# The first tile pair of a matrix product: A's rows by halves on both hardware queues, B's two tiles in column pieces by the software queue with a cast

## Chip, core and metric

The kernel runs on one core of a Trainium2 chip. The metric is the device time of one execution in microseconds (us); of the kernel before, eight runs are shown and their median is taken.

## What is computed

```python
def reference(a, b, gamma, eps):          # a, b: 2048 x 2048 fp32, gamma: 2048 fp32
    x = np.matmul(a, b)
    rms = np.sqrt(np.mean(x ** 2, axis=-1, keepdims=True) + eps)
    return (gamma * x / rms).astype(np.float32)
```

## The kernel before

**Tiles.** The 2048 rows of A make 16 row blocks of 128. The contraction of 2048 is cut into 16 tiles of 128 (`kt`), taken in 8 pairs (`kp`), so one pair covers 256 columns of A and 256 rows of B. The 2048 columns of B are two halves (`j`) of 1024. `raw[j][kp]` holds one pair of B for one half: 128 partitions, 2 tiles, 1024 columns, in bf16. A matmul takes a transposed 128x128 tile of A and 512 columns of B.

**The order of work is written out by hand** (`manual_schedule`): every engine runs its instructions in program order. There are three stages.

1. *The head.* Row blocks 0 to 3 times the left half of B, streamed by `kp`: 8 groups of (row block, 512 columns), of which seven keep a PSUM bank and the eighth is summed in parts (`stream_in_parts`, L415). For each `kp`, `stream` issues 14 matmuls (L384), and `transpose_head(kp + 1)` puts the next pair's 8 transposes (L172) in the middle of them; DVE copies the transposed tiles into `head_at` (L177).
2. *The right half of B* for the same four row blocks, again by `kp`.
3. *Row blocks 4 to 15* in pairs, with seven products in the place of eight (Strassen's scheme, L289), while ACT and DVE square, normalise and store earlier blocks.

**Who loads what.** `load_head(kp)` issues, on GpSimd's software queue, the pair of A for four row blocks (`early<-in_a_dram`, L105, 512 KB of fp32 read, cast to bf16) and the pair of B (`b<-in_b_dram`, L99, 1 MB of fp32 read, cast to bf16). The software queue has eight completion semaphores in turn, so the ninth load waits until the first has landed, the tenth until the second, and so on. Below, A1, B1, A2, ... are these loads for `kp` = 1, 2, ...

**The first pair (`kp` = 0) is loaded in another way.** A0 is one fp32 load on SP's hardware queue (L91), and B0's left half is two fp32 loads, one for each tile, on ACT's hardware queue (L93). They land in `a0f` and `b0f`, two parts of the tile `early`. `transpose_first` transposes A0 in fp32 on PE (L155, against `identity_f`, which GpSimd builds after it has issued A1 and B1), moves the result to `head_at` on DVE (L161), and casts B0 into `raw[0][0]` with DVE and ACT, half the columns each (L158, L160). The other loads of the head are issued by GpSimd before, between and after these.

Eleven matmuls on a zero tile (L145) keep PE busy until the first data come.

Of the kernel before, what the change touches and what calls it, by code (L numbers as in the profile page):

```python
# [8 lines left out]
FP32 = mybir.dt.float32  # L9
# [8 lines left out]
def kernel(  # L18
# [13 lines left out]
    nc = tc.nc  # L32
    P = 128
# [4 lines left out]
    W2 = 2 * P  # L38
    MB = M // P
    CH = 512  # L40
    NCH = N // CH
    HALF = N // 2
    HB = 4
# [15 lines left out]
    early = consts.tile([P, 6 * 2048], BF16, name="early")  # L59
    head_at = consts.tile([P, KT, HB, P], BF16, name="head_at")  # L60
    raw = [[consts.tile([P, 2, HALF], BF16, name=f"b_{j}_{kp}") for kp in range(KP)]
           for j in range(2)]
# [2 lines left out]
    sums = [t_left, t_right]  # L65

    a0f = early[:, 0:2048].bitcast(FP32).rearrange("p (r k) -> p r k", r=HB)
    b0f = [early[:, 2048 + t * 2048:2048 + (t + 1) * 2048].bitcast(FP32) for t in range(2)]
    NAH = 6
    ah_slot = [early[:, 6144 + s * 1024:6144 + (s + 1) * 1024].rearrange("p (r k) -> p r k", r=HB)  # L70
               for s in range(NAH)]
# [16 lines left out]
        return (at_even, at_odd)[(mb // 2) % 2][:, mb % 2]  # L88


    nc.sync.dma_start(out=a0f, in_=a[0:HB * P, 0:W2].rearrange("(r p) k -> p r k", p=P))  # L91
    for t in range(2):
        nc.scalar.dma_start(out=b0f[t], in_=b[t * P:(t + 1) * P, 0:HALF])  # L93

    def ah(kp):
        return ah_slot[(kp - 1) % NAH]

    def load_b(j, kp):
        nc.gpsimd.dma_start(  # L99
            out=raw[j][kp],  # L100
            in_=b[kp * W2:(kp + 1) * W2, j * HALF:(j + 1) * HALF].rearrange(
                "(t p) n -> p t n", p=P))

    def load_head(kp):
        nc.gpsimd.dma_start(  # L105
            out=ah(kp),
            in_=a[0:HB * P, kp * W2:(kp + 1) * W2].rearrange("(r p) k -> p r k", p=P))
        load_b(0, kp)
# [15 lines left out]
    def wait_for(src):  # L124

        nc.gpsimd.tensor_copy(out=pace, in_=src)

    load_head(1)
    identity_f = t_left[:, 2, KP - 1, 0:2 * P].bitcast(FP32)
    make_identity(nc, identity_f)  # L130
# [19 lines left out]
    def transpose_first():  # L150
        bank = [ps_t.tile([P, CH], FP32, name="tbank"), ps_a.tile([P, CH], FP32, name="acc")]
        view = [b.rearrange("p (r m) -> p r m", r=HB) for b in bank]
        for t in range(2):
            for r in range(HB):
                nc.tensor.matmul(view[t][:, r, :], a0f[:, r, t * P:(t + 1) * P], identity_f,  # L155
                                 is_transpose=True, start=(r == 0), stop=(r == HB - 1))
        for t in range(2):
            cast_first = [lambda: nc.vector.tensor_copy(out=raw[0][0][:, t, :CH],  # L158
                                                        in_=b0f[t][:, :CH]),
                          lambda: nc.scalar.copy(out=raw[0][0][:, t, CH:], in_=b0f[t][:, CH:])]  # L160
            move = [lambda h=h: nc.vector.tensor_copy(  # L161
                out=head_at[:, t, 2 * h:2 * h + 2, :], in_=view[t][:, 2 * h:2 * h + 2, :])
                for h in range(2)]
            for work in (cast_first + move if t == 0 else move + cast_first):
                work()

    def transpose_head(kp):
        bank = ps_t.tile([P, CH], FP32, name="tbank")
# [263 lines left out]
    for r in range(HB):  # L432
        x_tile(r, 0)
    early_sums = {4: ((2,), 0, 6), 5: ((5,), 0, 7), 6: ((1,), 0, KP)}
    transpose_first()
    for kp in range(KP):
        if kp + 4 < KP:
# [393 lines left out]
```

## Time and profile before

| | |
|---|---|
| median of 8 runs (lowest to highest) | 222.68 us (222.32 to 222.78) |
| the profiled execution: its time, its span | 222.68 us, 220.9 us |
| PE busy | 209.5 us, 95% of the span |
| DVE, ACT, POOL busy | 167.4, 128.0, 29.4 us |
| mean granted TensorE clock | 0.989 |
| software queue (q0): packets, MB | 9936, 23.33 |
| SP's hardware queue (q1), ACT's (q10): MB | 22.29, 1.31 |
| loads of B by POOL: count, KB written each, median issue to landing | 15, 512, 17.3 us |

The span is what the profile covers; about 1.8 us of the time lie around it. Start times in the profile count from the span's start. The DMA view counts bytes as written, so a load that casts fp32 to bf16 counts half of what it reads. A row of the timeline gives start, duration, engine, source line, operation, what is written and read, count, and in brackets the idle time just before it and what ended that. POOL is GpSimd, PEld is the weight load of a matmul; POOLq, SPq and ACTq are the issuing queues.

### The profile page before, as it was taken

How to read it: one execution, taken by the hardware profiler on the slowest of the kernel's cores; microseconds unless marked ns; L12 is line 12 of the kernel's file. 1: busy time of each engine (PE TensorE's matmuls, PEld its weight loads, DVE VectorE, ACT ScalarE, POOL GpSimd, SP SyncE). 2: the span in 40 equal slices, each digit the busy share in tenths (PEclk: the TensorE clock that was granted, in tenths of full speed). 3: DMA queues.
4: the chain of work that ended last, by engine and by line, in shares of the span. 5: the costliest groups of instructions: out<-in, count | busy, mean ns of one | idle time of the engine just before them, and what ended most of it. 6: DMA issues, size and time to landing. Idle time of an engine off the chain costs nothing.

```text
span 220.9 us, 3022 instructions
## 1 busy us (share of the span) xinstructions
PE 209.5 (95%) x1035; PEld 97.7 (44%) x1035; DVE 167.4 (76%) x330; ACT 128.0 (58%) x263; POOL 29.4 (13%) x59
## 2 busy tenths in 40 slices
PE   7899899999999999999999999999999999999950
PEld 2445444444455444444444444444444444444430
DVE  2428789999988898959697639855794759797691
ACT  3110002830698898479855997299738995334570
POOL 7634233220000002200010002000200000000040
PEclk9999999999999999999999999999999999999995
DMA  6999999999938595945799249955799349044045
GB/s 187 221 202 209 203 205 212 211 211 234 426 121 355 198 294 129 332 197 119 235 297 402 104 88 269 355 229 95 191 291 375 72 89 384 27 190 193 1 191 190
DMA packets 36321, 47.13 MB, mean 213 GB/s; under 512 B 21969, under 2 KB 26065, under 8 KB 34897
## 3 DMA queue, kind: packets, MB, share of 16 engines
q0 software_dynamic: 9936, 23.33, 41.6%
q1 hardware_dynamic: 25936, 22.29, 33.4%
q10 hardware_dynamic: 432, 1.31, 2.0%
q8 instruction: 8, 0.13, 0.2%
q14 instruction: 9, 0.07, 0.1%
HBM read 34.60 MB, written 16.78 MB: 233 GB/s over the span
## 4 chain that ended last, share of the span: by engine, by line
PE 83%; DMA 8%; POOL 3%; DVE 2%; issue 1%; ACT 1%; DVEq 0%; ACTq 0%; POOLq 0%
PE acc L289 69%; PE acc L384 12%; DMA b<-in_b_dram 8%; POOL early L105 1%; POOL b L99 1%; DVE x L709 1%; PE tbank L415 1%; PE tbank L172 1%; DVE x L712 1%; ACT sq L307 0%; PE tbank L189 0%; PE acc L189 0%; DVE a L709 0%; ACT sq L778 0%; DVE x L786 0%
## 5 line engine op out<-in xcount | busy, mean ns | idle before, releaser
L289 PE MATMUL acc<-b,s 128*128 128x512 bf16 x408 | 92.1, 379 | 0.0
L289 PEld LDWEIGHTS <-s 128*128 128x128 f16 (+1 forms) x512 | 49.9, 98 | 59.9 <-DVE s L264 0.4
L384 PE MATMUL acc<-b,head_at 128*128 128x512 bf16 x176 | 41.8, 379 | 0.8 <-DMA b<-in_b_dram 0.7
L307 ACT ACTIVATE sq<-x 128x512 bf16<-128x512 f32 x54 | 34.0, 630 | 6.9 <-DVE x L709 3.0
L366 DVE SCALAR_TENSOR_TENSOR x<-x,r,gamma_sb 128x1024 f32<-128x1024 f32 x28 | 34.8, 1281 | 0.7
L223 ACT ACTIVATE sq<-a 128x1024 bf16<-128x1024 f32 x24 | 25.3, 1054 | 3.2 <-DMA a<-in_a_dram 2.7
L384 PEld LDWEIGHTS <-head_at 128*128 128x128 bf16 x176 | 16.8, 98 | 20.3 <-issue 1.5
L246 ACT ACTIVATE head_at<-a,s 128x2048 f16<-128x2048 f32 x10 | 20.0, 1998 | 3.7 <-DVE s L233 3.7
L426 ACT COPY x<-acc 128x512 f32<-128x512 f32 x6 | 3.4, 588 | 25.4 <-PE acc L384 25.4
L289 PEld LDWEIGHTS <-head_at 128*128 128x128 f16 (+1 forms) x112 | 11.0, 98 | 13.2
L289 PE MATMUL acc<-early,head_at 128*128 128x512 bf16 x64 | 14.5, 379 | 0.0
L289 PEld LDWEIGHTS <-at_even 128*128 128x128 f16 x96 | 9.4, 98 | 11.3
L289 PE MATMUL acc<-early,s 128*128 128x512 bf16 x56 | 14.4, 379 | 0.0
L264 DVE TENSOR_TENSOR s<-head_at 128x1024 f16<-128x1024 f16 (+5 forms) x22 | 13.4, 637 | 0.1
L596 DVE TENSOR_TENSOR x<-x,x 128x512 f32<-128x512 f32 x9 | 6.2, 692 | 8.8 <-ACT x L594 8.3
L99 POOL DMA_DIRECT2D b<-in_b_dram x15 | 10.6, 706 | 15.9 <-DMA b<-in_b_dram 13.3
L578 ACT COPY x<-acc 128x512 f32<-128x512 f32 x9 | 5.2, 573 | 11.5 <-PE acc L289 7.6
L289 PE MATMUL acc<-t_left,s 128*128 128x512 bf16 x48 | 11.3, 379 | 0.0
L280 DVE TENSOR_TENSOR b<-b 128x1024 bf16<-128x1024 bf16 x16 | 10.9, 692 | 0.2
L289 PE MATMUL acc<-early,at_even 128*128 128x512 bf16 x48 | 10.8, 379 | 0.0
L289 PE MATMUL acc<-t_left,head_at 128*128 128x512 bf16 x48 | 10.8, 379 | 0.0
L289 PE MATMUL acc<-t_left,at_even 128*128 128x512 bf16 x48 | 10.8, 379 | 0.0
(111 smaller groups left out, 216.6 us busy)
## 6 DMA issues: line engine op xcount, KB each, us to landing
out_dram<-x SPq DMA_DIRECT2D x30, 512.0 KB, 3.8
a<-in_a_dram POOLq DMA_DIRECT2D x10, 1024.0 KB, 8.7
b<-in_b_dram POOLq DMA_DIRECT2D x15, 512.0 KB, 17.3
a<-in_a_dram POOLq DMA_DIRECT2D x4, 512.0 KB, 16.6
early<-in_a_dram POOLq DMA_DIRECT2D x7, 256.0 KB, 14.7
early<-in_b_dram ACTq DMA_DIRECT2D x2, 512.0 KB, 6.0
gamma_sb<-in_gamma_dram POOLq DMA_DIRECT2D x1, 1024.0 KB, 14.8
early<-in_a_dram SPq DMA_DIRECT2D x1, 512.0 KB, 5.6
```

Of the source, the lines that this page charges most:

```text
L99: nc.gpsimd.dma_start(out=raw[j][kp], in_=b[kp * W2:(kp + 1) * W2, j * HALF:(j + 1) * HALF].rearrange("(t p) n -> p t n", p=P))
L223: nc.scalar.activation(out=junk, in_=a32[mb][:, h * HALF:(h + 1) * HALF], func=ACTF.Square, scale=2.0 ** -8, accum_out=n2[:, h:h + 1])
L246: nc.scalar.activation(out=a16[mb], in_=a32.pop(mb), func=ACTF.Copy, scale=factor.pop(mb))
L264: nc.vector.tensor_tensor(out=sum_of(g, s)[:, lo:hi, :], in0=x[:, lo:hi, :], in1=y[:, lo:hi, :], op=op)
L280: nc.vector.tensor_tensor(out=flat[:, 1:3, :], in0=flat[:, 1:3, :], in1=flat[:, 0::3, :], op=ALU.add)
L289: nc.tensor.matmul(bank, lhsT[:, kp, :], rhs, start=(start and kp == 0), stop=(kp == KP - 1), skip_group_check=not start)
L307: nc.scalar.activation(out=sq[:, 0:CH], in_=src, func=ACTF.Square, scale=inv_sqrt_n, accum_out=msq[mb][:, c:c + 1])
L366: nc.vector.scalar_tensor_tensor(out=x, in0=x, scalar=inverse_of[mb], in1=gamma_sb[:, h * HALF:(h + 1) * HALF], op0=ALU.mult, op1=ALU.mult)
L384: nc.tensor.matmul(bank, head_at[:, kt, r, :], head_rhs(c, kt), start=(kt == 0), stop=(kt == KT - 1))
L426: copy(out=x_chunk(*g), in_=banks[g])
L578: nc.scalar.copy(out=c, in_=one[1])
L596: nc.vector.tensor_tensor(out=t, in0=t, in1=x12, op=ALU.add)
```

## The change

A0 becomes two loads of 256 KB, row blocks 0 and 1 on SP's queue and row blocks 2 and 3 on ACT's. B0 no longer passes through `b0f`: four loads on the software queue, ahead of `load_head(1)`, each 256 columns of both tiles, are cast to bf16 on the way into `raw[0][0]`. The casts by DVE and ACT go, and ACT takes the moves to `head_at` of the second tile, which DVE had.

```diff
-    b0f = [early[:, 2048 + t * 2048:2048 + (t + 1) * 2048].bitcast(FP32) for t in range(2)]
...
-    nc.sync.dma_start(out=a0f, in_=a[0:HB * P, 0:W2].rearrange("(r p) k -> p r k", p=P))
-    for t in range(2):
-        nc.scalar.dma_start(out=b0f[t], in_=b[t * P:(t + 1) * P, 0:HALF])
+    for h, queue in enumerate((nc.sync, nc.scalar)):
+        queue.dma_start(out=a0f[:, 2 * h:2 * h + 2, :],
+                        in_=a[2 * h * P:(2 * h + 2) * P, 0:W2].rearrange("(r p) k -> p r k", p=P))
...
+    for c in range(4):
+        col = slice(c * W2, (c + 1) * W2)
+        nc.gpsimd.dma_start(out=raw[0][0][:, :, col],
+                            in_=b[0:W2, col].rearrange("(t p) n -> p t n", p=P))
     load_head(1)
     identity_f = t_left[:, 2, KP - 1, 0:2 * P].bitcast(FP32)
     make_identity(nc, identity_f)
...
-        for t in range(2):
-            cast_first = [lambda: nc.vector.tensor_copy(out=raw[0][0][:, t, :CH],
-                                                        in_=b0f[t][:, :CH]),
-                          lambda: nc.scalar.copy(out=raw[0][0][:, t, CH:], in_=b0f[t][:, CH:])]
-            move = [lambda h=h: nc.vector.tensor_copy(
-                out=head_at[:, t, 2 * h:2 * h + 2, :], in_=view[t][:, 2 * h:2 * h + 2, :])
-                for h in range(2)]
-            for work in (cast_first + move if t == 0 else move + cast_first):
-                work()
+        for t, copy in enumerate((nc.vector.tensor_copy, nc.scalar.copy)):
+            for h in range(2):
+                copy(out=head_at[:, t, 2 * h:2 * h + 2, :], in_=view[t][:, 2 * h:2 * h + 2, :])
```

The matmuls and transposes on PE keep their number and order. After the change GpSimd issues four loads more before it builds `identity_f`, and the ninth load of the software queue is A3 in the place of A5.

## Prediction

> **What bounds the kernel now.** PE is busy for 95% of the span, so I first read the chain of waits: it should be PE work to the end, and the question is where it begins. By line, and in order of time:
>
> ```profile
> PE 83%; DMA 8%; POOL 3%; DVE 2%; issue 1%; ACT 1%; DVEq 0%; ACTq 0%; POOLq 0%
> ```
> ```profile
> 6.69 0.65 POOL early L105
> 7.35 17.46 DMA b<-in_b_dram
> 24.80 0.04 issue
> 24.84 1.67 PE acc L384 x7
> 26.52 0.45 PE tbank L172 x8
> ```
>
> From 24.84 us to about 208 us PE waits for nothing of length. Before that the end is not set by PE's start at 7.6 us, but by one load of B, landing at 24.80. The timeline shows the same from PE's side:
>
> ```profile
> 6.46 0.63 PE L155 MATMUL tbank<-t_left,early 128*128 128x128 f32 x4 [0.94 <-DMA early<-in_a_dram]
> 7.61 2.81 PE L384 MATMUL acc<-b,head_at 128*128 128x512 bf16 x12
> 11.65 0.59 PE L415 MATMUL tbank<-b,head_at 128*128 128x512 bf16 x2 [0.35 <-DVE head_at L177]
> 12.28 1.67 PE L384 MATMUL acc<-b,head_at 128*128 128x512 bf16 x7
> ...
> 24.84 1.67 PE L384 MATMUL acc<-b,head_at 128*128 128x512 bf16 x7 [0.71 <-DMA b<-in_b_dram]
> ```
>
> A `kp` takes PE 3.90 us (starts at 12.28, 16.18, 20.07). The next would be 23.97; it is 24.84, so 0.87 us are lost to B4. The trace's landing records give B1 12.24, B2 16.02, B3 19.96, B4 24.80, B5 28.62, B6 32.54, B7 36.37, against PE's starts 12.28, 16.18, 20.07, 24.84, 28.74, 32.64, 36.54: PE runs 0.04 to 0.17 us behind the software queue all through the head. On the right half of B the last landing, 56.25, is followed by its use at 56.40. So the head is paced by the **software queue**, and PE gains from an earlier start only what that queue gains.
>
> Third, the DMA view by stretches: 0 to 8 us, 2 to 6.3 us, then 8 to 12 us (columns: packets, MB written, share of 16 engines).
>
> ```profile
> q10 hardware_dynamic: 278, 1.04, 46.6%
> q1 hardware_dynamic: 528, 0.52, 19.8%
> q0 software_dynamic: 99, 0.05, 4.6%
> ```
> ```profile
> q10 hardware_dynamic: 181, 0.68, 55.8%
> q1 hardware_dynamic: 528, 0.52, 36.8%
> ```
> ```profile
> q0 software_dynamic: 849, 0.81, 122.8%
> q10 hardware_dynamic: 10, 0.01, 0.8%
> ```
>
> GpSimd issues A1 at 1.25 us, yet until 6.3 us q0 has moved nothing (first packet in the records at 6.53), and until 8 us only 0.05 MB. A0 and B0, as fp32 on the hardware queues, hold the engines until 8.0 us. After that q0 runs at 0.81 MB in 4 us, 0.203 MB/us.
>
> **What the Trainium skill says.** "DMA: Bandwidth & Descriptors", section Issuing engines are not separate DMA queues: loads from all queues run on the same 16 engines and interleave. The trace agrees on the sharing, but q0 gets no packet from 2 to 6.3 us, so here hardware queues go first; I use the measurement. Same page, SWDGE vs HWDGE vs iDMA: only the software queue casts. The trace agrees: B0 on ACT's queue is fp32 and needs L158 and L160. "SBUF — State Buffer", section SBUF: two separate sides: DVE's wide copies can block GpSimd from writing descriptors. I see none of it: the issue at 5.63, beside DVE's cast, took 0.73 us, others 0.70.
>
> **The change part by part.**
>
> *The software queue's stream (sets the end).* Before, its bulk begins at 8.0 us with 0.05 MB done, as if it had begun at 8.0 - 0.05/0.203 = 7.75. After, the hardware queues carry only A0, 0.52 MB. From 0 to 4.3 us they moved 0.6 MB before, ramp included (the packet records reach 0.52 MB at about 4.1), so I take 4.1 us as their end; 3.7 if 1 KB rows go at 0.3 MB/us, as from 4.3 to 6.3, from 2 us on, 4.6 if the ramp is longer. Then q0 carries B0: 0.524 MB at 0.203, 2.6 us, and A1 follows at 6.7. The stream is ahead by 7.75 - 6.7 = **1.05 us** (1.45 to 0.55). The source of the gain: B0 as fp32 on ACT's queue moved 0.33 MB from 6.3 to 8 us, about 0.2 MB/us as written, no faster than q0, which writes half the bytes for it.
>
> *Supply on q0.* Issues start at 1.25, 2.18, 2.88, 3.58 (pitch of L105 and L99 before: 0.93 for the first, then 0.70); A1 4.28, B1 5.04. On idle engines q0's first packet came 1.3 us after its issue (issue 64.04, packet 65.36), so each is ready before 6.4. A2 moves from 3.42 to 6.3, B2 to 7.1, A3 and B3 to about 8 to 9, A4 and B4 to about 10 and 11. A3 to B4 now wait for the four pieces, landed by 7.4; A5 waits for A1 as before. q0 needs A2 only at 6.7 + 3.9 = 10.6. Free.
>
> *`identity_f`.* GpSimd builds it after four more issues: 2.86 us later by the pitches, 3.47 + 2.86 = 6.33. A0 lands well before (6.33 in the landing records before, sharing with B0; now some 4.6). The first transposes start at 6.4 instead of 6.46. Cost nothing; what was covered by A0 is now the limit. PE is idle from 5.5 to 6.4 as it was.
>
> *Moves and casts.* DVE's two casts (0.71, 0.43 us) and ACT's two (0.62 each) go. The cast of B0's second tile ended at 9.3, and PE's matmuls show a 0.05 us gap there: gain 0.05. DVE's moves of the first tile (0.38 us each) follow the transposes as before; ACT's two, estimated at 0.4 us from L160's 0.62 for 512 columns, run at 7.2 to 8.0 and are wanted at 8.8, when the seventh group takes their bank, and 9.0. Free.
>
> *PE's start.* Transposes at 6.4 put the first matmul at 7.55 against 7.61. It needs pieces 0 and 1, the next also 2 and 3: last byte at 6.7, plus 0.7 (B1's last byte at 8.0 + (0.786 - 0.05)/0.203 = 11.6, landing 12.24) is 7.4. With the 0.05 gap and B1's wait (0.2) gone, PE could reach `kp` 4 at 24.84 - 0.87 - 0.2 - 0.05 - 0.06 = 23.66, 1.18 us sooner; B4's landing allows 24.80 - 1.05 = 23.75. The loads decide: 1.05 us, later slacks (0.10 to 0.17 us) add nothing. SP's queue has nothing else until the first store, and ACT's has one load less.
>
> *Sum.* Against the profiled execution, 222.68 us with a span of 220.9 and equal to the median: 222.68 - 1.05 = **221.6 us**. PE's own limit bounds the gain at about 1.25.
>
> **The rivals.** *A: the software queue starts late by itself* (slower). That q0 carries nothing before 6.53 us might not be the hardware queues' doing, but a first start that takes 5.3 us. B0 then has no other way in. q0's bulk begins at about 6.5, B0 is through at 9.1, the stream is 9.1 - 7.75 = 1.35 us late, the first matmul comes at 9.8: 224.0 us. It decides from the point where q0's bulk begins after 5.15 us (7.75 - 2.6). For it: no first start without hardware traffic is in the trace, and at 6.5 us q0 ran beside q10 while at 5 us it didn't beside q1. Against it: an issue at 88.96, beside stores on q1, got its first packet after 4.4 us, while quiet ones took 1.3. 16 in 100.
>
> *B: the stream gains little.* A0 by halves ramps more slowly and holds the engines until 4.7 to 5.15 us, or GpSimd's pieces take 0.93 us each like the first issue, so `identity_f` comes at 7.0 and PE's own start gives back half. Gain 0 to 0.45: 222.3 to 222.7. For it: 0.2 MB was all that moved before 3.3 us. Against it: that stretch was mostly 4 KB rows. 11 in 100.
>
> *C: the change as described does not happen*, as when the pieces were issued behind A1: the program shows them first on POOL. No share.
>
> **How the numbers follow.** A measurement of this kernel can tell about 0.2%, 0.45 us, from no change. Forecast, faster by 0.45 to 1.4 us: 73 in 100. B within 0.2%: 11. A slower by over 0.2%: 16. The forecast's own range is 221.3 to 222.2. The range reaches into A, whose mild cases (bulk at 5.6 to 5.7) give 223.2, and is cut below at 221.2, just past PE's limit: 221.2 to 223.2.
>
> **What would show it.** Right: q0's first packets at about 4 us and hardware traffic gone by then, B0's pieces landed by 7.4, A1 landed near 8.7 (before 9.71), PE's first matmul near 7.5, PE at `kp` 4 near 23.8 with a short wait or none, and the same 184 us from there to the end. Wrong: q0 silent until 6 us with idle engines; a matmul wait for a piece of B0 past 8.6 us; `identity_f` past 7 us; or a new wait behind `kp` 4, which would take the gain back later.

## The result, and the profile after

The changed kernel takes 223.88 us (median of 11 runs, 223.40 to 225.06) against 222.52 us (31 runs): ratio 1.007, 95% interval 1.0056 to 1.0084. It is slower by 1.4 us where 1.05 us less was forecast.

Its runs form two groups. The six at 223.4 to 223.9 us have a mean granted TensorE clock of 0.988 to 0.994; those at 224.7 to 225.1 have 0.980 or 0.981. One run lies outside this pairing, 224.57 us at 0.991, so a low clock is not all that can make a run long. The profiled execution is of the second group: 224.68 us, span 222.9 us. It took 2.00 us more than the profiled execution before.

The chain of waits by engine, of the changed kernel, and the same chain in order of time (start, duration):

```profile
PE 90%; DVE 3%; DMA 2%; POOL 1%; ACT 1%; issue 1%; DVEq 0%; ACTq 0%; POOLq 0%
```
```profile
1.24 2.21 POOL b L129 x3
3.45 0.12 issue
3.57 5.54 DMA b<-in_b_dram
9.11 0.05 issue
9.15 4.23 PE acc L381 x11
```

DMA's share fell from 8% to 2%, but the load that now sets PE's course is B0 itself. The fourth piece is issued at 3.57 us and lands at 9.11. After it the chain is nearly all PE to the end; the wait at `kp` 4 is gone.

The timeline of PE:

```profile
6.41 0.66 PE L158 MATMUL tbank<-t_left,early 128*128 128x128 f32 x4 [0.28 <-POOL t_left masks.py:199]
6.90 0.60 PE L158 MATMUL acc<-t_left,early 128*128 128x128 f32 x4
7.58 0.39 PE L381 MATMUL acc<-b,head_at 128*128 128x512 bf16 x1
9.15 4.23 PE L381 MATMUL acc<-b,head_at 128*128 128x512 bf16 x11 [1.19 <-DMA b<-in_b_dram]
...
15.05 1.67 PE L381 MATMUL acc<-b,head_at 128*128 128x512 bf16 x7
```

The transposes now wait for POOL's identity, and the first matmul runs at 7.58 as forecast. The second needs columns 512 to 1023 and waits for them until 9.15. Then eleven matmuls take 4.23 us, where twelve took 2.81 before. The windows view shows why (after the busy times: granted clock, DMA share, GB/s):

```profile
8.00:10.00 2.00, 0.84 (x3) 0.30 (x4) 0.00 (x0) 0.18 (x1) 2.00 (x11) 0.80 1.38 198
10.00:12.00 2.00, 2.00 (x6) 0.71 (x5) 0.00 (x0) 0.00 (x0) 1.74 (x3) 0.50 1.15 208
12.00:14.00 2.00, 2.00 (x15) 1.13 (x14) 0.13 (x1) 0.00 (x0) 0.70 (x1) 0.84 1.34 202
```

From 10 to 12 us PE runs at half clock. The same stretch before, at full clock:

```profile
10.00:12.00 2.00, 1.65 (x14) 0.93 (x13) 0.69 (x1) 0.00 (x0) 0.77 (x1) 1.00 1.16 203
```

Between the end of its warm-up at 6.13 us and the second matmul at 9.15 PE was busy for about half of the time, 1.48 of 3.02 us; its longest pause there was 1.19 us.

The DMA view of the changed kernel from 0 to 8 us, from 4 to 8, and from 8 to 12 us:

```profile
q0 software_dynamic: 970, 0.47, 59.4%
q1 hardware_dynamic: 272, 0.26, 10.0%
q10 hardware_dynamic: 272, 0.26, 9.3%
```
```profile
q0 software_dynamic: 853, 0.41, 105.8%
```
```profile
q0 software_dynamic: 918, 0.81, 126.2%
```

The hardware queues are through early: A0's two halves have landed at 3.90 and 4.17 us. The software queue has its first packet at 3.41. But from 4 to 8 us it moves 0.41 MB, 0.10 MB/us; only from 8 us on does it reach 0.203. In the first stretch the engines are busy all the time (105.8%), so they aren't short of work: each packet takes longer. In the packet records one of 512 B takes 77 ns on average from 4 to 6 us and 90 ns from 6 to 8, against 60 ns from 8 to 10, and fewer of them overlap.

### The profile page after: what moved, and what is told of

Its sections match the earlier page's. It is cut to its first block, busy times and chain, and to the rows that moved or that the text cites. A ratio compares the mean times of both kernels' runs of the same rounds, so it can differ in the third digit from the quotient of the medians.

```text
span 222.9 us, 3025 instructions
## 1 busy us (share of the span) xinstructions
PE 211.6 (95%) x1035; PEld 98.2 (44%) x1035; DVE 165.4 (74%) x326; ACT 127.4 (57%) x263; POOL 32.2 (14%) x63
## 4 chain that ended last, share of the span: by engine, by line
PE 90%; DVE 3%; DMA 2%; POOL 1%; ACT 1%; issue 1%; DVEq 0%; ACTq 0%; POOLq 0%
PE acc L286 68%; PE acc L381 18%; DMA b<-in_b_dram 2%; PE tbank L412 2%; PE tbank L169 1%; POOL b L129 1%; DVE x L706 1%; DVE x L709 1%; ACT sq L304 0%; PE tbank L186 0%; PE acc L186 0%; DVE head_at L174 0%; DVE a L706 0%; ACT sq L775 0%; DVE x L783 0%
## 5 line engine op out<-in xcount | busy, mean ns | idle before, releaser
L381 PE MATMUL acc<-b,head_at 128*128 128x512 bf16 x176 | 43.6, 391 | 1.3 <-DMA b<-in_b_dram 1.2
L98 POOL DMA_DIRECT2D b<-in_b_dram x15 | 10.6, 709 | 14.9 <-DMA b<-in_b_dram 11.9
L174 DVE COPY head_at<-tbank 128x1024 bf16<-128x1024 bf16 x7 | 4.8, 686 | 8.7 <-PE tbank L169 8.7
L125 POOL COPY pace<-x 128x1 f32<-128x1 f32 x4 | 1.6, 412 | 65.9 <-DVE x L602 64.7
```

Of the source, the lines that this page charges most:

```text
L98: nc.gpsimd.dma_start(out=raw[j][kp], in_=b[kp * W2:(kp + 1) * W2, j * HALF:(j + 1) * HALF].rearrange("(t p) n -> p t n", p=P))
L174: nc.vector.tensor_copy(out=head_at[:, 2 * kp:2 * kp + 2, :, :], in_=view)
L381: nc.tensor.matmul(bank, head_at[:, kt, r, :], head_rhs(c, kt), start=(kt == 0), stop=(kt == KT - 1))
```

## Experiments

Landing times below are the last of a load's sixteen completions in the trace. "Stream" is how much later than before the last load of B's right half lands (56.25 us before). Where one time stands alone, the kernel ran once, and the time is set beside 222.68 us of the profiled execution before. What is read from such a run is its trace.

### Which part costs

**x7: the pieces without A0's halves.**

```diff
-    for h, queue in enumerate((nc.sync, nc.scalar)):
-        queue.dma_start(out=a0f[:, 2 * h:2 * h + 2, :], in_=...)
+    nc.sync.dma_start(out=a0f, in_=a[0:HB * P, 0:W2].rearrange("(r p) k -> p r k", p=P))
```

> The changed kernel with the other part alone: A0 as one load on SP's queue, the pieces of B0 on the software queue. A0 on one queue needs until about 4 us in the place of 3.7, still well before GpSimd has built the identity at 6.3 us; the pieces land near 9.1 to 9.5 us and the time is that of the changed kernel, 223.4 to 225 us. The two halves of A0 are then worth nothing in the changed kernel.

Measured: 223.88 us, ratio 1.0059 (1.004 to 1.0077), A0 landed at 4.09 us, the last piece at 9.96. The same median as the changed kernel: the pieces cost, and the halves of A0 give nothing beside them.

**x6: A0's halves without the pieces.**

```diff
-    nc.sync.dma_start(out=a0f, in_=a[0:HB * P, 0:W2].rearrange("(r p) k -> p r k", p=P))
+    for h, queue in enumerate((nc.sync, nc.scalar)):
+        queue.dma_start(out=a0f[:, 2 * h:2 * h + 2, :], in_=...)
     for t in range(2):
         nc.scalar.dma_start(out=b0f[t], in_=b[t * P:(t + 1) * P, 0:HALF])
```

> The kernel before with one part of the change: A0 by halves on both hardware queues, and B0 as fp32 behind it on ACT's queue, cast by DVE and ACT as before. If reading B0 is what is slow, at 0.2 MB/us as read, A0 can no longer hide beside it: the hardware queues end near 3.7 + 1.05/0.2 = 9 us against 8.0, the stream of the software queue comes 0.9 us later, the time is about 223.4 us. If the slowness of the pieces belongs to the software queue, B0 goes at 0.3 MB/us or more, the hardware queues end near 7.2 us and the time is about 221.9 us.

Measured: 223.37 us, ratio 1.0045 (1.002 to 1.007); B0's second tile landed at 10.39 us against 8.68 before. The loss of the first guess, but not by its reason: before the software queue began, ACT's queue moved 0.33 MB of B0 from 3.5 to 4.5 us. q0 got its first packets at 4.8 us, with 0.62 MB still to come on ACT's queue; from 5.5 to 6.5 us both together moved 0.12 MB. So neither reading of the expectation holds as written. Two things follow: the slowness falls on both queues and not on the software queue alone, and the hardware queue did not go first here, though the prediction assumed that it does.

**x12: only B0's second tile on the software queue, in one load.**

```diff
-    for t in range(2):
-        nc.scalar.dma_start(out=b0f[t], in_=b[t * P:(t + 1) * P, 0:HALF])
+    nc.scalar.dma_start(out=b0f[0], in_=b[0:P, 0:HALF])
...
+    nc.gpsimd.dma_start(out=raw[0][0][:, 1, :], in_=b[P:W2, 0:HALF])
     load_head(1)
...
-            for work in (cast_first + move if t == 0 else move + cast_first):
+            for work in (cast_first + move if t == 0 else move):
```

> The kernel before with only B0's second tile moved: A0 whole on SP's queue and B0's first tile as fp32 on ACT's queue as before, the second tile by one software load with a cast, ahead of A1, and its two casts gone. The hardware queues end near 5.9 us in the place of 8.0; PE starts at 7.6 as before and wants the second tile at 9.1. At full rate the stream is ahead by 8.0 - (5.9 + 1.3) = 0.8 us: 221.9 us. If the software queue's first 0.26 MB go at 0.11 MB/us, they take 2.4 us, the stream is 0.3 us late: about 222.9 us, with PE not waiting for the tile (it lands near 8.9).

Measured: 222.78 us, ratio 1.0009 (1.0002 to 1.0017). The second reading: the tile landed at 8.74 us, PE didn't wait for it, B1 landed at 12.61 against 12.24. Half the bytes by the software queue cost a fifth of the loss. No version here beats the kernel before.

### Why the pieces are slow

**x1: the first two row pairs swapped; x5: the pieces read from A; x8: a small load that touches B's rows first; x2: one load in the place of four.**

```diff
 x1   in_=b[W2:2 * W2, col] for the pieces, b[0:W2, ...] for B1, A's columns likewise
 x5   in_=a[HB * P:HB * P + W2, col].rearrange("(t p) n -> p t n", p=P)
 x8 + nc.sync.dma_start(out=early[:, 2048:2112]..., in_=b[0:W2, 0:16]...)   ahead of A0
 x2 - for c in range(4): ...
 x2 + load_b(0, 0)
```

> The changed kernel with the first two row pairs of the contraction swapped: the first pair is columns 256 to 511 of A with rows 256 to 511 of B, the second is the old first. (Row blocks 4 to 15 keep A's natural order, so their products for these two pairs mix the wrong operands; no instruction or size differs.) Theory PLACE: the first 256 rows of B read slowly, about 0.11 MB/us as written, wherever they stand in the order. Then the four pieces land by about 7.4 us (the prediction's rate) and it is B1 that takes twice its 2.5 us. Theory FORM: the pieces themselves (1 KB rows, 512 B written, four loads in a row) are slow: unchanged, last piece near 9.1 us. Theory FIRST: the first loads of the software queue are slow whatever they are: also unchanged, 9.1 us.

> The changed kernel with the four pieces read from A (rows 512 to 767, columns 0 to 1023) in the place of B's first rows; A's other loads have touched that matrix by then, those rows not. (B0's left half is so wrong data; sizes, row pitch and order are the same.) Theory TOUCH-B: the first megabyte read from the matrix B is slow, whoever reads it. Then the pieces move at 0.2 MB/us and land near 7 us, and B1, now the first read of B, takes 4.5 us in the place of 2.5. Theory PATTERN: a first read of 256 rows of 4 KB at 8 KB pitch is slow from any matrix: unchanged, last piece near 9.1 us.

> The changed kernel with one small load more, first on SP's queue: 64 bytes of each of B's first 256 rows, into a place that is not used. Theory TOUCH-B in its form by rows or pages: the touch takes the first-read cost, the pieces then move at 0.2 MB/us from 3.6 us on and land near 7 us. If it is bytes that are slow and not the first touch, nothing changes but some 0.3 us for the load itself: last piece near 9.1 to 9.4 us.

> The changed kernel with B0 as one software load of 256 rows x 1024 columns (4 KB rows read, 2 KB written), the same form as B1 to B7, in the place of the four pieces. Theory FORM: B0 lands at about 3.6 + 2.6 + 0.7 = 7 us, the stream is 1.0 to 1.5 us ahead of before, the time is about 221.5 us. Theories FIRST and PLACE: B0's 0.52 MB still take some 4.5 us from 3.5 us on and land near 9 us, the time stays near 223.4 us or above.

Measured, last landing of B0: x1 9.49 us, x5 9.38, x8 9.57, x2 9.17 (the changed kernel: 9.11). x1, x5 and x8 ran once each: 224.14, 224.99, 224.99 us; x2 225.12 us, ratio 1.0127 (1.011 to 1.0144). From 4 to 8 us of x5, and from 4 to 7 of x2, the DMA view gives:

```profile
q0 software_dynamic: 873, 0.42, 100.8%
```
```profile
q0 software_dynamic: 185, 0.38, 101.6%
```

It is not these rows (x1), not the matrix (x5), not a first touch of the rows (x8, which touched 64 B of each), and not the 1 KB rows of the pieces (x2): a load of the form of B1 to B7 goes at 0.13 MB/us in this stretch. x2 is worse than the pieces in the median: four of its six runs had the clock near 0.98 (224.8 to 225.6 us), the other two took 223.3 and 223.6. PE's first matmul then waits for the whole of B0, from 6.4 to 9.21 us in its profile, which is of one of these two.

**x4: A1 ahead of the pieces; x9: A1 to A4 ahead of them; x10: GpSimd held back by six memsets, so that the software queue starts later.**

```diff
 x4 + nc.gpsimd.dma_start(out=ah(1), in_=a[0:HB * P, W2:2 * W2]...)     ahead of the pieces
 x9 + for kp in range(1, 5): load_a(kp)                                 ahead of the pieces
x10 + for n in range(6): nc.gpsimd.memset(x_slot[n], 0.0)               ahead of the pieces
```

> The changed kernel with A1's load (512 B written per row, as the pieces) issued on the software queue ahead of the four pieces of B0. Theory FIRST: A1 is now the slow one, 0.26 MB at about 0.11 MB/us, landing near 6.5 us, and the pieces speed up as time passes. Theory FORM or PLACE: A1 moves at 0.2 MB/us and lands near 5.6 us, and the four pieces still take 4.5 us, landing near 10.3 us. The time is in both cases longer than that of the changed kernel, by 1 us or more, since B0 comes later.

> The changed kernel with the loads A1, A2, A3 and A4 ahead of the four pieces of B0 on the software queue, so that the pieces move at about 9 us and later in the place of 3.6. Theory EARLY: what the software queue moves before 8 or 9 us is slow, whatever it is. Then the A loads are slow (0.11 to 0.16 MB/us) and the pieces, once the A loads are through, take 0.52/0.2 = 2.6 us. Theory FIRST-B: the first load of B's form is slow (0.11 MB/us, 4.5 us) whenever it comes. The whole is much longer than the changed kernel (by 5 us or more), since B0 comes last.

> The changed kernel with six memsets of 128x1024 fp32 on GpSimd ahead of the pieces, so that the software queue's very first load starts several us later, with nothing else in flight. If slow is a window in time from the kernel's start (to 8 or 9 us), the pieces now move at 0.2 MB/us. If slow is the first use of the queue (its first 4 to 5 us), they move at 0.11 MB/us as before. Longer than the changed kernel by the delay.

Measured: x4, 224.53 us: A1 landed at 6.77, the last piece 3.9 us later: first in line is slow, and the pieces behind it still are. x9, 230.62 us: A4 landed only at 11.90, 1.05 MB in over 8 us, and the four pieces 2.7 us after it, at full rate (first fence below, 11.9 to 14 us). x10, 229.36 us: first packets after 7.5 us, the pieces landed from 9.14 to 14.17. The second fence has 8 to 13 us of x10:

```profile
q0 software_dynamic: 628, 0.41, 134.3%
```
```profile
q0 software_dynamic: 1152, 0.56, 102.6%
```

0.11 MB/us, long after the time at which the changed kernel was at full rate. So no clock time ends the slowness, and the form of B0 is not its cause (x9). What these runs share is that the slow stretch follows the software queue's first packets: it lasts from them to about 8 us in the changed kernel (4.6 us) and to about 12 us in x9 (8.5 us, with one faster microsecond in between). x10 has a second one, from about 15 to 18 us, after a microsecond at full rate.

**x11, x13, x14: GpSimd quiet while B0 moves.** x11 keeps the four pieces; x13 has one load; x14 is x13 with memsets in the place of rest.

```diff
-    load_head(1)
     ...
     make_identity(nc, identity_f)
 x14 + for n in range(7): nc.gpsimd.memset(x_slot[n % 4], 0.0)
+    nc.gpsimd.tensor_copy(out=quiet, in_=raw[0][0][:, 1, HALF - 1:HALF])
+    load_head(1)
```

> The changed kernel with GpSimd building the identity right behind the pieces and then waiting until the last piece has landed, before it issues A1, B1 and the rest: while the pieces move, GpSimd writes no descriptors. Theory DESCRIPTORS: writing descriptors for the next loads slows the engines' work on the pieces; then they move at 0.2 MB/us from 4.5 us on and land by about 7 us. Otherwise they still land near 9 us. The time is longer than the changed kernel's, since A1 and B1 are issued late.

> The changed kernel with B0 as one software load (one issue of 0.9 us), then the identity, then GpSimd idle until B0 has landed; A1, B1 and the rest follow. While B0 moves, no descriptor at all is written. Theory DESCRIPTORS (the engines are slow while GpSimd writes descriptors): 0.52 MB at 0.2 MB/us from 3.6 us, landing near 7 us, against 9.17 us for the same load with GpSimd writing on. Theory START (the software queue's loads are slow for some us after it begins from rest): landing near 8.5 to 9 us all the same. The time is longer than the changed kernel's, since A1 is issued late.

> As the run before it (B0 as one software load, the rest of the loads held back until it has landed), with seven memsets of 128x1024 fp32 on GpSimd while B0 moves, in the place of rest. If any writing by GpSimd slows the engines, B0 lands as late as beside descriptor writing, near 9 us. If it is the descriptors, B0 lands as in the run before it.

Measured: last landing of B0 in x11 8.19 us, in x13 9.06, in x14 8.97; times 228.81, 231.25, 229.99 us, mostly because A1 and B1 come late (B1 lands at 17.48, 19.57 and 18.67 us). The row of GpSimd that waits for B0 in x13:

```profile
9.12 0.18 POOL L131 CAST quiet<-b 128x1 f32<-128x1 bf16 x1 [6.38 <-DMA b<-in_b_dram]
```

For 6.38 us GpSimd writes no descriptor, and the load is as slow as in x2 (9.17). That descriptor writing slows the engines falls as the whole cause. As a part of it, it doesn't fall: the first of the load's sixteen completions came at 6.46 us against 7.34 in x2, and x11 was 0.9 us quicker than the changed kernel. With one trace of each, how much of that is chance stays open. After the rest the queue starts again; A1 is then quick, and B1 is slow again: it lands 6.8 us after A1 in x13 and 5.8 in x14, against 2.5 before.

**x15: the kernel before, with the software queue at rest until the hardware queues are done.**

```diff
+    for n in range(7): nc.gpsimd.memset(x_slot[n % 4], 0.0)
     load_head(1)
```

> The kernel before with seven memsets of 128x1024 fp32 on GpSimd ahead of A1's load, so that the software queue is at rest until about 7.5 us, while A0 and B0 are on the hardware queues as before. If it is the start of the software queue that slows all 16 engines, the hardware queues, which ended at 8.0 us in the kernel before, now end near 6 to 6.5 us, and B0's second tile moves at 0.3 MB/us or more in the place of 0.2. If the two are independent, the hardware queues end at 8.0 us again. The time is longer by the delay of A1, some 5 us.

Measured: 225.81 us. The DMA view from 5.5 to 7 us, x15 first, then the kernel before:

```profile
q10 hardware_dynamic: 126, 0.46, 75.4%
q1 hardware_dynamic: 37, 0.03, 5.9%
```
```profile
q10 hardware_dynamic: 74, 0.30, 78.2%
q1 hardware_dynamic: 51, 0.04, 9.0%
```

With no software load issued, ACT's queue moves 0.46 MB where it moved 0.30, and B0's second tile lands at 7.48 us in the place of 8.68. The hardware queues end at about 7.1 us, between the two times of the expectation. So issuing loads on the software queue slows the hardware queues too, though q0 moves almost nothing in this stretch; whether it is the waiting loads or the writing of their descriptors, this run doesn't tell. When q0 then begins, for the first time in this kernel, A1 is quick (first packet 8.60, landed 10.79) and B1 lands 5.4 us later. A first start, then, does not make the very first load slow in every case.

### The clock

**x3: a longer warm-up.**

```diff
-    for _ in range(11):
+    for _ in range(16):
         nc.tensor.matmul(warm_bank, warm[:, 0:P], warm[:, 0:CH], start=True, stop=True)
```

> The changed kernel with 16 matmuls on the zero tile in the place of 11, so that PE stays busy until about 7 to 8.3 us. Theory GATE: the changed kernel's runs fall into two groups, near 223.4 and near 224.9 us, because in some executions PE's wait for B0 falls into a window in which its clock is cut to half. With the longer warm-up nearly all runs are in the lower group: median about 223.4 (223.3 to 223.8), no granted clock of 0.98. Rival: the two groups have another cause; then both stay and the median is 223.9.

Measured: 224.06 us (223.52 to 224.12, four runs), ratio 1.0057 (1.0042 to 1.0072), clocks 0.99 to 0.994. None of the four has a clock near 0.98, as forecast, and the profile has no half clock:

```profile
9.71 2.55 PE L381 MATMUL acc<-b,head_at 128*128 128x512 bf16 x11 [0.88 <-DMA b<-in_b_dram]
```

Eleven matmuls take 2.55 us, not 4.23. But x7, with the short warm-up, had no such run in five either, so four runs don't show that the longer warm-up removed the group. Nor does the length of PE's wait decide it: x7's profile has a wait of about 2.0 us before the second matmul and x2's one of 2.8 us before the first, both at full clock to the end of the head, while the changed kernel's 1.19 us was followed by half clock. The median is 0.65 us above the lower group, which was not forecast; in its profile the last piece lands at 9.66 and the stream is 1.41 us late.

### What sets the end

| execution | stream later | PE at `kp` 4 later | time longer |
|---|---|---|---|
| x12 | 0.53 | 0.05 | 0.52 |
| x7 | 1.04 | 1.07 | 1.19 |
| x3 | 1.41 | 0.85 | 1.36 |
| x1 | 1.45 | 0.60 | 1.46 |
| x2 | 0.26 | 0.48 | 0.59 |
| x6 | -0.35 | 0.79 | 0.75 |
| changed kernel | 0.73 | 1.91 | 2.00 |

All in us against the profiled execution before (PE's start at `kp` 4: 24.84). In every row the time follows the larger of the two within 0.15 us. The profiles that are not in the table do so too: x4, x8 to x11 and x13 to x15 within 0.11, x5 within 0.20. So the prediction's frame, a race of the stream against PE's own course, holds.

## Why the prediction was wrong

**The step that failed** is the term "q0 carries B0: 0.524 MB at 0.203, 2.6 us". The rate was read from 8 to 12 us, when the queue was under way. In its first stretch, from 4 to 8 us of the changed kernel, it was 0.10 MB/us: from q0's first packet at 3.41 to the last landing at 9.11 B0 took 5.7 us; the sum had 3.3 from 4.1 to 7.4. A1 then lands at 10.44 in the place of 9.71, so the stream is 0.73 us late and not 1.05 early. The trace before couldn't show the price: there the queue's first 1.5 us of packets lay beside the tail of ACT's loads.

**The second failure** is a cost that the prediction did not have: a late B0 was priced only by its delay. In the profiled execution, PE's second matmul comes 1.32 us later (9.15 against 7.83). From there to `kp` 1 takes 5.90 us; with the full clock it takes 4.21, as x3 shows, so half clock costs 1.69. The gaps that the prediction wanted to remove, 0.05 and 0.2 and then 0.87 us at `kp` 4, did go: 1.32 + 1.69 - 0.25 - 0.87 = 1.89, measured 1.91. Without the half clock PE would be 0.2 us late and the stream, 0.73, would decide. The lower group of runs, 0.9 us above the median before, is near that; no profile of it was kept, so this part is not shown.

**Two readings that were off.** The 0.87 us at `kp` 4 were read as a limit of the queue, but they come from a part of the engines being late: B4's sixteen completions run from 23.25 to 24.80 us, B3's from 19.42 to 19.96. With B3's spread B4 would have landed at about 23.8, an estimate from these figures, before PE's own 23.97. A 16 KB instruction fetch lies between, 0.98 us from 21.39 us on; that it is the cause is not shown. And rival B had 0.2 MB moved before 3.3 us; the packet records have 0.26. Neither changes the step that failed.

**What was right.** GpSimd's pitches put the identity at 6.33; it ended at 6.35. The first matmul was forecast at 7.55 and came at 7.58. A0 landed at 4.17, before the identity. The hardware queues ended sooner than the 4.1 us assumed (last packet 3.80), and q0's first packet came at 3.41, beside their last 0.05 MB. So far as this kernel goes the order was right; x6 shows that it is not a rule. Nobody waited for ACT's moves. The wait at `kp` 4 disappeared.

**The rivals.** A gave 224.0 us and the measured time is 223.88, but not by its mechanism: q0 was not silent until 6.5 us; it began at 3.41 and was slow. Its doubt, that a first start of this queue has a price which the trace doesn't show, was the right one; it had 16 in 100. The evidence taken against it, first packets 1.3 us after an issue on idle engines, tells of latency and nothing of rate. B's mechanisms did not occur.

**What stays open** is why the start is slow. Rows, matrix, row size, a touch of the rows and clock time are excluded by x1, x5, x2, x8 and x10. GpSimd's descriptor writing alone doesn't explain it (x13), although in x11, x14 and x15 the rate was back at 0.2 MB/us within 2 us of the end of GpSimd's run of issues (15.3, 16.1 and 14.6 us); the changed kernel was at full rate from 8 us on while GpSimd still issued, until 11.7. A1 was quick and B1 behind it slow at the first start in x15 and after the rest in x11, x13 and x14, for which no run has a reason. What decides whether PE falls to half clock is open as well.

## What to carry to other kernels

Take a queue's rate for the place where it will be used: the software queue moved about half as much in its first microseconds of the changed kernel as later, and no steady-state row shows that. When work is moved to a queue that has so far started behind cover, ask what its own start costs. And where PE waits for the first data, ask for the clock too: in the profiled execution a second matmul that came 1.3 us late was followed by another 1.7 us lost at half clock, and only some runs show it.

## What the runs showed of the hardware

- After the software queue's first packets there was a slow stretch of 4 to 9 us with 0.10 to 0.14 MB/us as written, against 0.20 later (changed kernel, x2, x5, x9, x10). In x15 the first load went at full rate and the slow stretch began with the second.
- The slow stretch falls on a hardware queue as well: 0.33 MB in 1 us by ACT's queue before q0's first packet, 0.12 MB in 1 us by both after it (x6).
- Where loads had been issued on the software queue, ACT's queue was slower although they moved almost nothing: 0.30 against 0.46 MB in 1.5 us (before and x15, one run).
- The 16 engines don't stay together: in x13 the completions of one load of 1 MB read spread from 6.46 to 9.06 us, and PE waits for the last. In the kernel before, the spread is 0.42 to 0.54 us up to A4's load and 1.55 to 1.70 from B4 on.
- Half clock in the head comes in stretches of 3.41 us (changed kernel, x5, x8, x11, x14, x15), or two or three times that (6.83 in x10 and x13, 10.24 in x9).
